# Removal keys' norms over 72 columns, and small matmuls tied behind the main passes in a two-layer RWKV-7 decoder kernel

## Chip, cores and metric

The kernel runs on one core of a Trainium2 chip. The metric is the device time of one execution in microseconds. TensorE (PE) does the matmuls and loads their weights (PEld), VectorE (DVE), ScalarE (ACT) and GpSimd (POOL) the elementwise work, and SyncE (SP) issues most transfers.

## The reference

Two layers are applied to 288 tokens: a prompt of 256 and eight samples of 4. Each layer is a half-step SwiGLU feed-forward block, a mixer, and another feed-forward block, each behind an RMS norm with shift, scale and gate from a conditioning vector. The mixer adds a causal pooling branch and an RWKV-7 branch. What matters here is how RWKV-7 normalises its removal keys, one vector of 64 for each token and each of eight heads, and then runs its recurrence:

```python
kk = hs((k * k_k).astype(f32))
kk = kk / jnp.maximum(jnp.sqrt(jnp.sum(kk * kk, axis=-1, keepdims=True)), 1e-12)
...
S = S * w_t[:, :, None, :] + sa[..., None] * b_t[:, :, None, :] + v_t[..., None] * k_t[:, :, None, :]
y = jnp.einsum('bhvk,bhk->bhv', S, r_t)
```

Here `a_t` is minus the normalised key and `b_t` the normalised key times `a`.

## The kernel before

**Layout.** Features lie on the 128 partitions and the 288 tokens along the free axis. A width of 512 is four tiles, so one tile holds two heads, and `HP` is 4. The prompt is worked on in four chunks of 64 tokens.

**Main passes.** Every large product is made of weight tiles of 128x128 from one list (`weight_order`). `split_strip` takes four tiles at a time and splits each weight into a high part `wh` (ACT, L225) and a low part `wl` (DVE, L226). `mm3` (L251) then runs three matmuls a tile: `wh` by the high and by the low part of the data, and `wl` by the high part. They are called main passes below. Each is tied behind the one before by `tc.issue_after(self.last.ins)`, so among themselves they run in the order of the list. Results land in PSUM tiles `psmm` (three) and `pswk` (four). One list step of the mixer (`step`) is two weight tiles, that is six main passes.

**The planner.** The program is written as one sequence, and a planner then lays it out on the engines by its own durations: on each engine the earliest written instruction that it takes to be ready goes next. `tc.high_priority(offset=75)` moves the splits, and the evictions of the mixer's main passes, 75 instructions ahead in that ranking. An engine runs its list strictly in the planned order; where a true duration is longer than the planned one, it waits.

**The mixer.** It weaves two sequences. The main sequence (`main_ops`) holds the projections left after the first five tiles, the gates and the branch products. The other holds small products: low-rank weights (L814), squared norms of the removal keys (L835), their spread over the partitions of a head (`head_spread`, L819), scores (L906), transposes (L918), a triangular inverse (DVE, L937 to L949, then L1196 and L1208), the chunk recurrence (L1268 to L1286), outputs (L1244, L1248) and their group norm, and the final transposes (L1255). Small products go to `pswk` tiles, and nothing ties them to main passes: the planner may place them ahead of main passes written earlier, or behind ones written later.

`fill()` takes its next count from `PLAN` and runs that many items: first from a queue, then, where that is empty, main steps. `add` puts a small product into the queue with three main steps behind it. The counts are used up in this order: one at L829, four in the loop of the key norms (L836), one each at L846, L894, L1183, L1192, L1204 and L1211, then two in each of four chunks (L1270, L1282; entries 11 to 18), then entry 19 at L1304, behind `outputs(1)` of the last half of the prompt, and four at L1312. At the end of chunk 1, nine entries are added to an empty queue (L1297 to L1300). What follows the chunks is

```python
outputs(1)
fill()
while queue:
    fill(1)
need(10)
...
transposed(1)
```

where `fill(1)` takes one item and no entry of `PLAN`.

**The key norms.** For each `j` of four tiles ACT squares the keys, and a matmul with `hs` (128x32; column `e` sums the 64 rows of head `e`) writes 32 rows of one PSUM tile, of which two are used, by 288 tokens. ACT takes the root of the whole tile into `rn` (L838), DVE the maximum with 1e-12 (L839) and the reciprocal (L843), each on 128 partitions by 288 columns. Then `head_spread(rn, j)` multiplies by `hb` (32x128) and gives each head's value to its 64 partitions, from which DVE forms the scaled keys `AR` and `BK` (L878 to L891). `head_spread` serves the bonus sums `bsum` as well. The scores (L906) read `AR` and `BK`, and DVE masks them into `MM` (L910). Evictions of main passes by DVE (L668) and the splits of `wl` (L226) are queued between all of these.

Of the kernel before, what the change touches and what calls it, by code (L numbers as in the profile page):

```python
# [20 lines left out]
AF = mybir.ActivationFunctionType  # L21
# [4 lines left out]
P = 128  # L26
# [6 lines left out]
NT = TP + NS  # L33
DEPTH = 2
H = 8
HP = 4
# [32 lines left out]
WEAVE = 3  # L69
PLAN = (1, 0, 0, 11, 1, 15, 14, 18, 5, 6, 2, 0, 12, 13, 4, 4, 3, 9, 13, 1, 2, 8, 4, 2, 3, 0, 5, 1, 1, 7)  # L70
FIRST = 3
# [65 lines left out]
for _n, _w in PARAMS:  # L137
# [3 lines left out]

CONSTS = [("ones", 1), ("eps", 1), ("ident", 128), ("mhalf", 1), ("hs", 32), ("hb", 128),
          ("maskp", 128), ("masks", 64), ("bmask", 8), ("id32", 32), ("id16", 16), ("halves", 2), ("scan", 288),
# [8 lines left out]
def make_consts():  # L152
# [6 lines left out]
    p = np.arange(P)  # L159
    put("ident", np.eye(P, dtype=np.float32))  # L160
    put("mhalf", np.full((P, 1), -0.5, np.float32))
    put("ones", np.ones((P, 1), np.float32))
    hs = np.zeros((P, 32), np.float32)
    hb = np.zeros((P, P), np.float32)
    for e in range(2):
        hs[64 * e:64 * e + 64, e] = 1.0
        hb[e::32, 64 * e:64 * e + 64] = 1.0
    put("hs", hs)
    put("hb", hb)
    s, t = p % 64, np.arange(64)  # L170
    put("maskp", np.stack([s[:, None] < t, s[:, None] <= t], 1).astype(np.float32))
    s, t = p % 32, np.arange(32)
# [14 lines left out]


class Kernel:
    def __init__(self, ctx, tc, io):  # L190
        self.ctx, self.tc, self.nc, self.io = ctx, tc, tc.nc, io
        self.order = weight_order()
        self.wpos = 0
        self.nstrips = len(self.order) // STRIP
        self.raw, self.hl = {}, {}
        self.next_slot, self.next_split = 0, 0
        self.psn = 0
        self.last = None

    def pool(self, name, bufs=1, **kw):  # L200
# [54 lines left out]

    def ps_wk(self):
        return self.p_wk.tile([P, 512], F32, tag="wk", name="pswk")

# [364 lines left out]
    def mixer(self, l):  # L623
        nc = self.nc
        tc = self.tc
        V, S, G, T = nc.vector, nc.scalar, nc.gpsimd, nc.tensor
        self.mod_close()
# [9 lines left out]
        def tj(name):  # L637
            return tl([P, NT], "tj", name, bufs=3)
# [18 lines left out]
        rks = tl([P, HP, 32], "rks")  # L657
        G.tensor_tensor(out=rks, in0=self.cst("hs").unsqueeze(1).to_broadcast([P, HP, 32]),
                        in1=self.par(l, "r_k").unsqueeze(2).to_broadcast([P, HP, 32]), op=ALU.mult)
        V.tensor_scalar(ka1, self.par(l, "k_a"), -1.0, 1.0, op0=ALU.mult, op1=ALU.add)  # L660
        ident, hs, hb = self.cst("ident"), self.cst("hs"), self.cst("hb")

# [154 lines left out]
        def head_spread(rows, j):  # L817
            ps = self.ps_wk()
            T.matmul(ps[:, :NT], hb[32 * j:32 * j + 32, :], rows[32 * j:32 * j + 32, :], start=True, stop=True)  # L819
            return ps[:, :NT]  # L820

        halves = [slice(0, 64), slice(64, 128)]
        quarter = [slice(32 * g, 32 * g + 32) for g in range(4)]
# [6 lines left out]
        kps = self.ps_wk()  # L830
        for j in range(HP):
            lora_mm(j)
            t = tl([P, NT], "tj", "kk2", bufs=3)
            S.activation(out=t, in_=xk[:, j, :], func=AF.Square, scale=self.par(l, "k_k", j))
            T.matmul(kps[32 * j:32 * j + 32, :NT], hs, t, start=True, stop=True)  # L835
            fill()  # L836
        rn = tj("rn")
        S.activation(out=rn, in_=kps[:, :NT], func=AF.Sqrt)  # L838
        V.tensor_scalar(rn, rn, 1e-12, None, op0=ALU.max)  # L839
# [36 lines left out]
        for j in range(HP):  # L876
            ps = head_spread(rn, j)
# [5 lines left out]
        for j in range(HP):  # L883
            t = tj("ka")
# [55 lines left out]
        for s in range(30, 0, -1):  # L940
            t0 = (s + 1) // 2
            n = 16 - t0
# [44 lines left out]
        out = []  # L987
# [205 lines left out]
        ps = self.ps_wk()  # L1193
        for u in range(16):
            for q in range(2):
                T.matmul(ps[hi[q], 32 * u:32 * u + 32], MU[lo[q], u, q, 0, 32:64], Tc[lo[q], u, :],  # L1196
                         start=True, stop=True)
# [7 lines left out]
        ps = self.ps_wk()  # L1205
# [8 lines left out]
        for q in range(2):  # L1214
            ps = self.ps_wk()
# [7 lines left out]
            n = 1 + q  # L1223
# [285 lines left out]
```

## Time and profile before

| | us |
|---|---|
| median of 3 runs | 1427.91 |
| the three runs | 1427.98, 1427.91, 1426.09 |
| profiled execution | 1426.15 |
| its span, first to last instruction | 1424.4 |
| PE busy in it | 1379.7 |
| DVE busy | 958.6 |
| ACT busy | 724.4 |

The profile comes from one execution. Its span leaves out 1.75 us around the first and last instruction. An engine's idle time is listed just before the instruction that ended it, with the instruction elsewhere that released it. The end of a matmul is modelled, so lines of PE overlap. A matmul of plain f32 data appears as two records; a main pass is one. PEclk is the granted clock of PE as a share of 2.4 GHz.

### The profile page before, as it was taken

The numbers are of one execution on the slowest core, as the hardware profiler recorded it, in microseconds if no ns is written. First come the engines' busy times: TensorE is split into PE (matmuls) and PEld (weight loads), VectorE is DVE, ScalarE is ACT, GpSimd is POOL, SyncE is SP. The second block draws the span as 40 slices with busy tenths as digits, with TensorE's granted clock in tenths as the row PEclk, the third lists the DMA queues.
The fourth block names the chain that finished last, engine by engine and source line by source line (L and its number), as shares of the span: only waits on it lengthen the run. The fifth ranks groups of instructions, "written<-read, shape, count | busy, mean of one in ns | idle before, by whom it ended". The sixth has DMA issues, their size and how long they took to land.

```text
span 1424.4 us, 28726 instructions
## 1 busy us (share of the span) xinstructions
PE 1379.7 (97%) x11280; PEld 1286.5 (90%) x11280; DVE 958.6 (67%) x2071; ACT 724.4 (51%) x1466; POOL 106.8 (7%) x151
## 2 busy tenths in 40 slices
PE   6999999999999999999999999999999999999997
PEld 5989999988888999899999899997897889999997
DVE  4644556899867885455677555669996678755554
ACT  4444444686534664444455445457654356555532
POOL 0000002000112010000211000110001210100012
PEclk9999999999999999999999999999998999999999
DMA  8878865543323776887667644554341247445552
GB/s 363 312 267 308 296 237 179 183 148 113 100 92 135 253 255 221 303 302 264 244 212 273 238 148 163 165 187 143 114 145 63 90 153 276 154 163 163 165 172 97
DMA packets 70264, 279.74 MB, mean 196 GB/s; under 512 B 9328, under 2 KB 11504, under 8 KB 60784
## 3 DMA queue, kind: packets, MB, share of 16 engines
q1 hardware_dynamic: 66384, 274.33, 54.7%
q10 hardware_dynamic: 3744, 3.57, 0.9%
q8 instruction: 88, 1.44, 0.4%
q14 instruction: 48, 0.39, 0.1%
HBM read 273.64 MB, written 4.23 MB: 195 GB/s over the span
## 4 chain that ended last, share of the span: by engine, by line
PE 86%; DVE 9%; issue 2%; DMA 1%; ACT 1%; POOL 1%; POOLq 0%; DVEq 0%; ACTq 0%; SPq 0%
PE psmm L251 44%; PE pswk L251 30%; PE psmd L315 4%; DVE wl L226 2%; PE pswk L918 1%; DVE xn L495 1%; DMA raw<-in_wflat 1%; DVE ul L498 0%; DVE pw L688 0%; POOL gn L1128 0%; DMA shs<-in_shift 0%; PE pswk L1273 0%; PE pswk L814 0%; DVE MM L910 0%; DMA cc<-in_c 0%
## 5 line engine op out<-in xcount | busy, mean ns | idle before, releaser
L226 DVE TENSOR_TENSOR wl<-raw,wh 128x512 fp32r<-128x512 f32 x732 | 512.4, 702 | 331.5 <-ACT wh L225 323.9
L225 ACT CAST wh<-raw 128x512 fp32r<-128x512 f32 x732 | 452.8, 620 | 543.1 <-PE psmm L251 284.6
L251 PE MATMUL psmm<-uh,wh 128*128 128x288 f32 x1072 | 324.2, 302 | 1.2 <-ACT uh L506 1.2
L251 PE MATMUL psmm<-ul,wh 128*128 128x288 f32 x1072 | 320.0, 298 | 0.4 <-DVE ul L507 0.3
L251 PE MATMUL psmm<-uh,wl 128*128 128x288 f32 x1072 | 319.4, 298 | 1.0 <-DVE wl L226 1.0
L251 PEld LDWEIGHTS psmm<-uh,wh 128*128 128x128 f32 x1072 | 203.6, 190 | 13.0 <-issue 8.2
L251 PEld LDWEIGHTS psmm<-uh,wl 128*128 128x128 f32 x1072 | 204.0, 190 | 4.7 <-issue 2.6
L251 PEld LDWEIGHTS psmm<-ul,wh 128*128 128x128 f32 x1072 | 203.9, 190 | 3.9 <-issue 2.3
L251 PE MATMUL pswk<-ul,wh 128*128 128x288 f32 x608 | 179.7, 296 | 0.0
L251 PE MATMUL pswk<-uh,wh 128*128 128x288 f32 x608 | 179.7, 296 | 0.0
L251 PE MATMUL pswk<-uh,wl 128*128 128x288 f32 x608 | 179.6, 295 | 0.0
L251 PEld LDWEIGHTS pswk<-uh,wh 128*128 128x128 f32 x608 | 114.7, 189 | 5.4 <-issue 4.2
L251 PEld LDWEIGHTS pswk<-ul,wh 128*128 128x128 f32 x608 | 114.7, 189 | 0.0
L251 PEld LDWEIGHTS pswk<-uh,wl 128*128 128x128 f32 x608 | 114.6, 189 | 0.0
L251 PE MATMUL pswk<-hl,wh 128*128 128x288 f32 x352 | 103.8, 295 | 0.0
L251 PE MATMUL psmm<-hl,wh 128*128 128x288 f32 x352 | 103.8, 295 | 0.0
L251 PE MATMUL psmm<-hh,wl 128*128 128x288 f32 x352 | 103.8, 295 | 0.0
L251 PE MATMUL pswk<-hh,wl 128*128 128x288 f32 x352 | 103.7, 295 | 0.0
L251 PE MATMUL psmm<-hh,wh 128*128 128x288 f32 x352 | 103.7, 295 | 0.0
L251 PE MATMUL pswk<-hh,wh 128*128 128x288 f32 x352 | 103.2, 293 | 0.0
L315 PE MATMUL psmd<-modw,csilu 128*32 128x512 f32 (+2 forms) x832 | 70.6, 481 | 9.1 <-DMA modw<-in_wmod 9.1
L378 POOL TENSOR_TENSOR sq<-x 128x288 f32<-128x288 f32 x28 | 19.8, 708 | 770.1 <-DVE x L533 770.1
(321 smaller groups left out, 2379.3 us busy)
## 6 DMA issues: line engine op xcount, KB each, us to landing
raw<-in_wflat SPq DMA_DIRECT2D x366, 512.0 KB, 3.4
modw<-in_wmod SPq DMA_DIRECT2D x72, 1024.0 KB, 7.3
s<-in_wkv SPq DMA_DIRECT2D x4, 512.0 KB, 6.7
o_wkvs<-s SPq DMA_DIRECT2D x4, 512.0 KB, 2.7
x<-in_x SPq DMA_DIRECT2D x1, 1152.0 KB, 5.4
o_y<-yo SPq DMA_DIRECT2D x2, 288.0 KB, 2.5
o_y<-yo ACTq DMA_DIRECT2D x2, 288.0 KB, 2.6
o_pool<-po SPq DMA_DIRECT2D x8, 67.5 KB, 2.7
```

The lines of the kernel that those rows point to most:

```text
L225: self.nc.scalar.copy(wh, src)
L226: self.nc.vector.tensor_tensor(out=wl, in0=src, in1=wh.bitcast(F32), op=ALU.subtract)
L251: self.last = self.nc.tensor.matmul(ps, w, x, start=start and n == 0, stop=stop and n == 2)
L315: mm = nc.tensor.matmul(self.mod_ps[32 * q:32 * q + 32, :size], self.csilu[:, k, :], w[:, kk, q, :], start=(k == 0), stop=(k == KD - 1))
L378: nc.gpsimd.tensor_tensor(out=t, in0=x, in1=x, op=ALU.mult)
L495: nc.vector.scalar_tensor_tensor(out=t, in0=self.x[:, k, :TP], scalar=g1, in1=r[:, :TP], op0=ALU.mult, op1=ALU.mult)
L918: T.transpose(ps[:n, 128 * hp:128 * hp + 128], src(hp), ident)
```

## The change

The squared norms are gathered in quarters. The 288 tokens are cut into four runs of 72, and run `t` of tile `j` goes to rows `2t` and `2t + 1` of the 32 rows of `j`, so that eight rows by 72 columns hold what two rows by 288 held. Four matmuls with four forms of `hs` add up in the same PSUM columns. Root, maximum and reciprocal then work on 72 columns. `head_spread` picks the rows of each run with four forms of `hb`; for `bsum`, which is 288 wide, it makes one matmul as before. The constants grow by 96 and 384 columns.

In the mixer, `T` becomes an `Ordered` object: the first matmul or transpose after each new `pswk` tile is tied behind the last main pass written so far. Entry 19 of `PLAN` goes from 1 to 6.

```diff
@@ -67,7 +67,7 @@
 SLOT = 8
 PRIO = 75
 WEAVE = 3
-PLAN = (1, 0, 0, 11, 1, 15, 14, 18, 5, 6, 2, 0, 12, 13, 4, 4, 3, 9, 13, 1, 2, 8, 4, 2, 3, 0, 5, 1, 1, 7)
+PLAN = (1, 0, 0, 11, 1, 15, 14, 18, 5, 6, 2, 0, 12, 13, 4, 4, 3, 9, 13, 6, 2, 8, 4, 2, 3, 0, 5, 1, 1, 7)
 FIRST = 3
 RMS = {0: 0.25, 1: 0.15, 2: 0.25}
 SPREAD = {0: 0.45, 1: 0.4, 2: 0.45}
@@ -139,7 +139,7 @@
     _o += _w
 NPAR = _o
 
-CONSTS = [("ones", 1), ("eps", 1), ("ident", 128), ("mhalf", 1), ("hs", 32), ("hb", 128),
+CONSTS = [("ones", 1), ("eps", 1), ("ident", 128), ("mhalf", 1), ("hs", 128), ("hb", 512),
           ("maskp", 128), ("masks", 64), ("bmask", 8), ("id32", 32), ("id16", 16), ("halves", 2), ("scan", 288),
           ("rc", 64)]
 COFF, _o = {}, 0
@@ -160,11 +160,12 @@
     put("ident", np.eye(P, dtype=np.float32))
     put("mhalf", np.full((P, 1), -0.5, np.float32))
     put("ones", np.ones((P, 1), np.float32))
-    hs = np.zeros((P, 32), np.float32)
-    hb = np.zeros((P, P), np.float32)
-    for e in range(2):
-        hs[64 * e:64 * e + 64, e] = 1.0
-        hb[e::32, 64 * e:64 * e + 64] = 1.0
+    hs = np.zeros((P, 4, 32), np.float32)
+    hb = np.zeros((P, 4, P), np.float32)
+    for t in range(4):
+        for e in range(2):
+            hs[64 * e:64 * e + 64, t, 2 * t + e] = 1.0
+            hb[2 * t + e::32, t, 64 * e:64 * e + 64] = 1.0
     put("hs", hs)
     put("hb", hb)
     s, t = p % 64, np.arange(64)
@@ -186,6 +187,27 @@
     return c
 
 
+class Ordered:
+
+
+    def __init__(self, kernel):
+        self.k = kernel
+
+    def _issue(self, f, *args, **kw):
+        k = self.k
+        if not k.fresh or k.last is None:
+            return f(*args, **kw)
+        k.fresh = False
+        with k.tc.issue_after(k.last.ins):
+            return f(*args, **kw)
+
+    def matmul(self, *args, **kw):
+        return self._issue(self.k.nc.tensor.matmul, *args, **kw)
+
+    def transpose(self, *args, **kw):
+        return self._issue(self.k.nc.tensor.transpose, *args, **kw)
+
+
 class Kernel:
     def __init__(self, ctx, tc, io):
         self.ctx, self.tc, self.nc, self.io = ctx, tc, tc.nc, io
@@ -196,6 +218,7 @@
         self.next_slot, self.next_split = 0, 0
         self.psn = 0
         self.last = None
+        self.fresh = False
 
     def pool(self, name, bufs=1, **kw):
         return self.ctx.enter_context(self.tc.tile_pool(name=name, bufs=bufs, **kw))
@@ -254,6 +277,7 @@
         return self.p_mm.tile([P, 512], F32, tag="mm", name="psmm")
 
     def ps_wk(self):
+        self.fresh = True
         return self.p_wk.tile([P, 512], F32, tag="wk", name="pswk")
 
     def ps_any(self):
@@ -623,7 +647,7 @@
     def mixer(self, l):
         nc = self.nc
         tc = self.tc
-        V, S, G, T = nc.vector, nc.scalar, nc.gpsimd, nc.tensor
+        V, S, G, T = nc.vector, nc.scalar, nc.gpsimd, Ordered(self)
         self.mod_close()
         es = ExitStack()
         pl = es.enter_context(tc.tile_pool(name=f"mx{l}", bufs=1, reuse_waits="tile"))
@@ -655,10 +679,11 @@
         V.tensor_tensor(out=shs, in0=shs, in1=self.par(l, "mu").unsqueeze(2).to_broadcast([P, NPA, NB]), op=ALU.mult)
         V.tensor_scalar(mu1, self.par(l, "mu"), -1.0, 1.0, op0=ALU.mult, op1=ALU.add)
         rks = tl([P, HP, 32], "rks")
-        G.tensor_tensor(out=rks, in0=self.cst("hs").unsqueeze(1).to_broadcast([P, HP, 32]),
+        G.tensor_tensor(out=rks, in0=self.cst("hs")[:, 0:32].unsqueeze(1).to_broadcast([P, HP, 32]),
                         in1=self.par(l, "r_k").unsqueeze(2).to_broadcast([P, HP, 32]), op=ALU.mult)
         V.tensor_scalar(ka1, self.par(l, "k_a"), -1.0, 1.0, op0=ALU.mult, op1=ALU.add)
-        ident, hs, hb = self.cst("ident"), self.cst("hs"), self.cst("hb")
+        ident = self.cst("ident")
+        hs, hb = [self.cst(n).rearrange("p (t m) -> p t m", t=4) for n in ("hs", "hb")]
 
         def shifted(i, ps, dst):
 
@@ -816,7 +841,10 @@
 
         def head_spread(rows, j):
             ps = self.ps_wk()
-            T.matmul(ps[:, :NT], hb[32 * j:32 * j + 32, :], rows[32 * j:32 * j + 32, :], start=True, stop=True)
+            r = quarter[j]
+            n = rows.shape[1]
+            for t in range(NT // n):
+                T.matmul(ps[:, n * t:n * t + n], hb[r, t, :], rows[r, :], start=True, stop=True)
             return ps[:, :NT]
 
         halves = [slice(0, 64), slice(64, 128)]
@@ -832,10 +860,13 @@
             lora_mm(j)
             t = tl([P, NT], "tj", "kk2", bufs=3)
             S.activation(out=t, in_=xk[:, j, :], func=AF.Square, scale=self.par(l, "k_k", j))
-            T.matmul(kps[32 * j:32 * j + 32, :NT], hs, t, start=True, stop=True)
+            for i in range(4):
+                T.matmul(kps[32 * j:32 * j + 32, :NT // 4], hs[:, i, :], t[:, NT // 4 * i:NT // 4 * (i + 1)],
+                         start=i == 0, stop=i == 3)
             fill()
-        rn = tj("rn")
-        S.activation(out=rn, in_=kps[:, :NT], func=AF.Sqrt)
+
+        rn = tj("rn")[:, :NT // 4]
+        S.activation(out=rn, in_=kps[:, :NT // 4], func=AF.Sqrt)
         V.tensor_scalar(rn, rn, 1e-12, None, op0=ALU.max)
         for j in range(HP):
             V.tensor_tensor_scan(out=cs[:, j, :], data0=self.cst("scan"), data1=sig[:, j, :], initial=0.0,
```

## Rows read from the trace of the kernel before

**Rows 1.** The page: busy time by engine; the chain that ended last

```profile
PE 1379.7 (97%) x11280; PEld 1286.5 (90%) x11280; DVE 958.6 (67%) x2071; ACT 724.4 (51%) x1466; POOL 106.8 (7%) x151
PE 86%; DVE 9%; issue 2%; DMA 1%; ACT 1%; POOL 1%; POOLq 0%; DVEq 0%; ACTq 0%; SPq 0%
```

**Rows 2.** Windows, layer 0: us; PE, PEld, DVE, ACT, POOL busy; clock; DMA

```profile
283.00:334.00 51.00, 47.50 (x354) 40.23 (x353) 49.85 (x124) 37.08 (x80) 1.04 (x2) 1.00 0.41 131
```

**Rows 3.** Lines, DVE: operation, shapes, count | busy us, mean ns

```profile
L413 DVE RECIPROCAL rb<-rb 128x144 f32<-128x144 f32 x10 | 9.8, 1020 | 0.6 <-ACT rb L409 0.6
L843 DVE RECIPROCAL rn<-rn 128x288 f32<-128x288 f32 x2 | 3.9, 1946 | 0.0
L839 DVE TENSOR_SCALAR rn<-rn 128x288 f32<-128x288 f32 x2 | 0.6, 304 | 0.0
```

**Rows 4.** Timeline, PE, scores of layer 0: start, us, instruction [idle before <-releaser]

```profile
320.50 0.29 PE L251 MATMUL psmm<-ul,wh 128*128 128x288 f32 x1
322.41 1.16 PE L906 MATMUL pswk<-AR,BK 64*128 64x128 f32 x16 [1.62 <-DVE AR L888]
324.08 0.40 PE L251 MATMUL psmm<-uh,wl 128*128 128x288 f32 x1 [0.51 <-DVE wl L226]
...
325.38 0.29 PE L251 MATMUL psmm<-uh,wl 128*128 128x288 f32 x1
325.60 2.06 PE L906 MATMUL pswk<-AR,BK 64*128 64x128 f32 x32
...
329.50 0.40 PE L251 MATMUL psmm<-uh,wh 128*128 128x288 f32 x1
...
330.68 0.65 PE L981 MATMUL pswk<-rkk,rks 128*32 128x288 f32 x2 [0.64 <-DVE rkk L975]
```

**Rows 5.** Timeline of DVE at layer 0's scores

```profile
321.05 1.22 DVE L888 TENSOR_TENSOR AR<-xr,ep 128x1024 f32<-128x1024 f32 x1
...
322.92 0.51 DVE L668 SCALAR_TENSOR_TENSOR sgl<-psmm,par,sgl 128x287 f32<-128x287 f32 x1
323.35 0.68 DVE L226 TENSOR_TENSOR wl<-raw,wh 128x512 fp32r<-128x512 f32 x1
```

**Rows 6.** Timeline of PE, layer 0: small products of f32

```profile
285.84 0.67 PE L835 MATMUL pswk<-kk,consts 128*32 128x288 f32 x2
...
310.04 0.77 PE L819 MATMUL pswk<-rn,consts 32*128 32x288 f32 x8
...
424.79 1.04 PE L1248 MATMUL pswk<-S,AR 128*64 128x128 f32 x8
...
436.25 1.10 PE L1244 MATMUL pswk<-UV,MM 128*64 128x64 f32 x32
```

**Rows 7.** Windows around falls of the clock, columns as in rows 2

```profile
373.30:376.60 3.30, 3.30 (x101) 2.96 (x101) 2.66 (x9) 3.20 (x6) 0.99 (x2) 1.00 0.12 19
...
1018.40:1021.70 3.30, 3.30 (x18) 3.02 (x20) 3.01 (x6) 1.06 (x2) 0.00 (x0) 0.53 0.18 29
...
1066.20:1069.50 3.30, 3.30 (x72) 3.12 (x72) 3.21 (x8) 1.52 (x3) 0.53 (x1) 0.53 0.04 11
1069.60:1079.70 10.10, 10.10 (x161) 8.85 (x162) 3.23 (x9) 4.22 (x8) 0.99 (x2) 0.50 0.17 54
```

**Rows 8.** Timeline of PE, both layers: stalls and what follows

```profile
370.62 1.20 PE L1196 MATMUL pswk<-Tc,MM 32*32 32x32 f32 x64 [1.78 <-DVE Tc L1189]
...
447.68 0.63 PE L1255 MATMUL pswk<-consts,yn 128*128 128x128 f32 x4 [2.79 <-DVE yn L1129]
...
1016.65 1.16 PE L906 MATMUL pswk<-AR,BK 64*128 64x128 f32 x16 [1.62 <-DVE AR L888]
...
1024.99 0.40 PE L251 MATMUL psmm<-uh,wh 128*128 128x288 f32 x1
...
1066.12 1.77 PE L1196 MATMUL pswk<-Tc,MM 32*32 32x32 f32 x64 [1.81 <-DVE Tc L1189]
...
1148.19 1.02 PE L1255 MATMUL pswk<-consts,yn 128*128 128x128 f32 x4 [2.78 <-DVE yn L1129]
```

## The prediction

> **What bounds the kernel now.** I read the page first: TensorE (PE) is busy for 1379.7 of 1424.4 us and makes 86% of the chain that ended last [rows 1]. So a change pays in three ways only: PE work removed, PE idle time filled, or PE time spent at the lower clock avoided. Work taken from VectorE (DVE) or ScalarE (ACT) counts where PE waits for it. The busy times by stretch come second. From 283 to 334 us, where layer 0's mixer builds its keys and scores, DVE is busy 49.85 of 51.0 us while PE has holes [rows 2]: here DVE decides. Third, the timeline around the changed lines. In layer 0 PE ends its main pass at 320.50 + 0.29 = 320.79, idles 1.62 us until DVE has written `AR` (L888), runs one score product (L906, sixteen matmuls), idles 0.51 us for a split weight `wl` (L226), runs ten main passes and then the second product [rows 4]. DVE takes its work in the order L888, L668, L226; that split ends at 323.35 + 0.68 = 324.03, just ahead of the pass that waited for it [rows 5]. Both idle times stand in layer 1 as well (the first shown in [rows 8]).
>
> Last, the clock. In layer 1 the granted clock is 0.53 from 1018.40, after that stall, and 0.53 and 0.50 from 1066.20 to 1079.70, after a stall of 1.81 us ahead of L1196; these are the lower level, 1.2 GHz [rows 7, 8]. The same stalls in layer 0, of 1.62 and 1.78 us, are followed by 1.00 [rows 2, 4, 7, 8]. A stall of this length may cost a fall or not; where it lies seems to matter, and so a shift of some us can trade one fall for another.
>
> **The norms over 72 columns.** The change puts the squared norms of 288 tokens into 72 columns, so three operations shrink. The reciprocal (L843) takes 1946 ns on 288 columns, and 1020 ns on 144 columns at L413 [rows 3]: 6.4 ns a column, so 72 columns give an estimate of 1020 - 72 x 6.4 = 557 ns, and 1.39 us are saved. The maximum (L839) takes 304 ns on 288; I take off 0.1 us. The root on ACT lies ahead of a queue that isn't full; I take 0. DVE does 1.5 us less in each layer, in the stretch where it is the bound.
>
> PE pays for it. Each of four key squares makes one product of two matmuls (L835), 0.67 us, and all four spreads of the result (L819) take 0.77 us [rows 6]; both become four pieces of 72 columns. That is 32 and 32 matmuls in place of 8 and 8. No row shows 72 columns, so bounds: below, nothing, because the columns add up to the same and 64-column matmuls come at 1.10 / 32 = 34 ns each; above, 128-column matmuls come at 1.04 / 8 = 130 ns each [rows 6], and 64 x 0.13 = 8.3 us stand against 4 x 0.67 + 0.77 = 3.45, so +4.9 us a layer. 72 is nearest to 64 columns, so I take +0.5 us. Where it falls matters more: both groups come before PE's wait at 320.79, which DVE ends, so up to 1.8 us of it (the wait worked out below) is hidden by that wait. I take 0 on the end; without that cover it is +0.5 a layer, at most +4.9.
>
> A rule speaks against this step. The Trainium skill, page "TensorE: Matmul & The Clock Gate", section "Back-to-back issue gap", says that the spacing of matmuls in a stream is set by the weight load as well, and gives 81 ns for 128 columns. Taken as a floor, 64 matmuls would cost 5.2 us against 3.45, an estimate of +1.7 us a layer. The 34 ns of the 64-column rows disagrees with it as a floor; those use different halves of the array side by side, which the new pieces don't. By the rule and without cover, the forecast below would be 3.5 us higher, 1428.0, which belongs to the first rival.
>
> The constants grow by 480 columns, 240 KB more in one load that is issued behind the first gates of the first layer, most of a feed-forward layer ahead of its first use. Transfers of all kinds are 1% of the chain [rows 1], and what hides this one is that layer. I take 0; without that cover it delays the weight loads behind it by a fraction of that 1%.
>
> **The tie of small products.** The first matmul after each new small PSUM tile must now follow the last main pass written before it. Counting passes in code and trace, only the first score product stands ahead of its written place, by the ten passes of [rows 4]; every other small product of both mixers already has as many passes ahead of it as the code writes, or more. So the tie acts there alone. It doesn't simply fill the hole: the ten passes want `wl`, and DVE splits it behind L888 and L668. PE will wait at 320.79 for `wl`. With DVE 1.5 us ahead, `wl` comes at 322.53 and the first pass at 322.58, an idle time of 1.79 instead of 1.62 + 0.51. From first pass to score product it is 325.60 - 324.08 = 1.52 us, and a product takes 2.06 / 2 = 1.03, so the second product starts at 322.58 + 1.52 + 1.03 = 325.13 instead of 325.60: 0.47 us gained a layer. What DVE waits for later, the first masking (L910), comes after 324.10 + 1.16 instead of 322.41 + 1.16; queued behind it are the other maskings and the bonus products, but further `wl` splits can go in that time, which now stand between the maskings. If that lets DVE run ahead, the 0.64 us that PE waits for `rkk` [rows 4] shrinks; bounds 0 and 0.64, I take 0.3.
>
> The stall is then one piece of 1.8 us, and in layer 1 begins some 0.5 us earlier for what layer 0 gained. I take it that the fall at 1018.40 goes. It costs (1024.99 - 1016.65) - (329.50 - 322.41) = 1.25 us [rows 4, 8].
>
> **More steps behind the outputs.** `PLAN[19]` goes from 1 to 6 at the `fill()` behind `outputs(1)`. The queue holds items there: nine entries with three steps each make 36, the four fills since took 4, 3, 9 and 13, so 7 are left. `fill` takes from the queue first, and the loop right behind empties it. One and then six, or six and then one, give the same sequence: this edit does nothing. The waits of 2.79 and 2.78 us for `yn` ahead of `transposed(1)` [rows 8] stay.
>
> **The sum.** -2 x (0.47 + 0.3) - 1.25 = -2.8 us. The profiled run took 1426.15 (span 1424.4 and 1.75 around it), so 1423.35. It is the second lowest of the four times known; the three runs shown average 1427.3, 1.2 above it, and the median is 1427.91. I forecast 1424.5, likely between 1422.5 and 1426.5. About 0.2%, 2.9 us, is what a measurement can tell from no change, so this lies just on the faster side.
>
> **Rivals.**
> *No net gain:* DVE's order leaves `wl` at about 323.0, and then the tie gives nothing, or the pieces are not covered and take back what it gives (2 x 0.5 up to 2 x 4.9). For it: DVE evicts main passes (L668) between the key steps, and those come at PE's pace, not earlier. Against: DVE has hardly any idle time to lose. About 1427.3. Chance 0.17.
>
> *The longer wait, slower:* the tie takes from PE the only work it had. If DVE's saving doesn't reach the split, `wl` stays at 324.03, the second product starts at 324.08 + 1.52 + 1.03 = 326.63, 1.03 late, the maskings and all behind them up to as much again, and a hole of 3.3 us brings the lower clock in layer 0 too, 1.25. From 1426.15: +2 x 2.06 + 1.25 = +5.4, with the 1.2 above 1432.7. It decides from `wl` at 325.60 - 1.52 - 1.03 - 0.05 = 323.0 on, that is if less than 1.0 of the 1.5 us arrives. Chance 0.15.
>
> *The long fall goes too:* the stall ahead of L1196 in layer 1 (1.81 us) shifts as in layer 0 and brings no fall. From L1196 to L1255 layer 0 takes 447.68 - 370.62 = 77.06 us and layer 1 1148.19 - 1066.12 = 82.07 [rows 8]: 5.0 us, so 1419.5. For it: the same stall without a fall stands in layer 0. Against: the shift must be of the right size, and layer 0 must not catch one. Chance 0.18.
>
> *The long fall comes to layer 0 as well:* the same mechanism the other way, +5.0, 1429.5. Chance 0.10. The skill's page above, section "Part 1: The HAM clock gate", says that the gate runs free of the kernel's start, by which neither trade could be told beforehand; the four times within 1.9 us rather speak for falls that come back at the same places.
>
> *The edit of the plan works:* were the queue shorter than I count, the tail waits would go, 2 x 2.79, giving 1418.9. Chance 0.04.
>
> **Chances.** The forecast has 0.36, about 0.22 of it under the bound for faster. Faster: 0.22 + 0.18 + 0.04 = 0.44. Same: 0.14 + 0.17 + 0.05 of the new fall = 0.36. Slower: 0.15 + 0.05 = 0.20. A range of 1418.5 to 1431.5 holds all but the longer wait beyond it and a spot at the low end.
>
> **What would show it.** L843 near 0.56 us and 72 columns in L838 and L839. In each layer no main pass between the first two score products, one wait of about 1.8 us for `wl` instead of two waits, and the second product about 0.5 us earlier. L835 and L819 four times as many, without PE waiting longer. The waits of 2.8 us ahead of the second L1255 unchanged in both layers. A clock of 1.00 after layer 1's scores. The forecast is wrong if `wl` comes after 323.0, if the planner, with other durations, moves main passes elsewhere, or if the long fall goes or doubles.

## The result, and the profile after

The changed kernel takes 1435.96 us (median of 7 runs, 1431.97 to 1436.59) against 1426.09 us beside it (7 runs, 1419.26 to 1427.98): ratio 1.0080, 95% interval 1.0057 to 1.0102. It is slower, by 9.9 us by the medians and 11.4 by the ratio; 1424.5 was forecast, and the time lies above the range. The profiled execution took 1436.44 us. First its page (busy time by engine) and the cores' view (span, mean granted clock):

```profile
PE 1389.1 (97%) x11376; PEld 1299.7 (91%) x11376; DVE 955.3 (67%) x2071; ACT 725.7 (51%) x1466; POOL 105.6 (7%) x151
```

```profile
core 0: 1434.7 us, clock 0.984
```

PE is busy 9.4 us longer than in [rows 1], so the loss isn't idle time alone: there is more work on PE, or it runs slower, and both will show. The timeline of PE at layer 0's spread (start, us, instruction), between two main passes:

```profile
312.52 0.29 PE L274 MATMUL psmm<-uh,wl 128*128 128x288 f32 x1
312.74 0.44 PE L202 MATMUL pswk<-rn,consts 32*128 32x72 f32 x2
313.02 0.49 PE L199 MATMUL pswk<-rn,consts 32*128 32x72 f32 x3
...
314.48 0.89 PE L199 MATMUL pswk<-rn,consts 32*128 32x72 f32 x8
315.30 0.40 PE L274 MATMUL psmm<-uh,wh 128*128 128x288 f32 x1
```

All small products of the mixer now carry the lines of the tie's helper (L202 with a tie, L199 without), so they are told by their tiles. The 32 matmuls of the spread take PE from 312.74 to 315.30, 2.56 us or 80 ns each, against 0.77 us for eight before [rows 6]. The key squares, cut into quarters just the same, took 0.67 us a product [rows 6] and now read

```profile
288.26 0.69 PE L199 MATMUL pswk<-kk,consts 128*32 128x72 f32 x8
```

So cutting by itself costs little. What DVE does behind it (line L249 is the split of `wl`, L693 the eviction of main passes, L919 the product `AR`):

```profile
318.68 0.69 DVE L249 TENSOR_TENSOR wl<-raw,wh 128x512 fp32r<-128x512 f32 x1 [0.98 <-ACT wh L248]
...
321.30 0.52 DVE L693 SCALAR_TENSOR_TENSOR xv<-psmm,par,xv 128x287 f32<-128x287 f32 x1 [1.83 <-ACT sho L692]
...
326.82 1.22 DVE L919 TENSOR_TENSOR AR<-xr,ep 128x1024 f32<-128x1024 f32 x1
...
328.36 0.68 DVE L249 TENSOR_TENSOR wl<-raw,wh 128x512 fp32r<-128x512 f32 x1
```

DVE, full in [rows 2], now idles 2.8 us, because it waits, by way of ACT, for main passes that PE delivers later: behind the pieces, and then at the lower clock (the window from 315.50 below). In the trace of pieces_only (the pieces alone, see below), where the clock doesn't fall there, DVE idles 1.35 and 0.57 us ahead of two evictions in this stretch. And PE at the scores and further on, with the waits that the tie and the outputs have (views of the timeline, by window; the rows from 1029.61 on are layer 1's scores):

```profile
329.10 0.40 PE L274 MATMUL psmm<-uh,wl 128*128 128x288 f32 x1 [2.21 <-DVE wl L249]
331.59 0.58 PE L202 MATMUL pswk<-AR,BK 64*128 64x128 f32 x1
...
375.82 0.21 PE L202 MATMUL pswk<-Tc,MM 32*32 32x32 f32 x1 [2.56 <-DVE Tc L1220]
...
458.96 0.35 PE L202 MATMUL pswk<-consts,yn 128*128 128x128 f32 x1 [2.79 <-DVE yn L1160]
...
1029.61 0.40 PE L274 MATMUL psmm<-uh,wl 128*128 128x288 f32 x1 [2.21 <-DVE wl L249]
...
1031.13 0.37 PE L202 MATMUL pswk<-AR,BK 64*128 64x128 f32 x1
...
1032.12 0.27 PE L202 MATMUL pswk<-AR,BK 64*128 64x128 f32 x1
```

In place of 1.62 and 0.51 us [rows 4] there is one wait of 2.21 us; the wait ahead of the products out of `Tc`, 1.78 and 1.81 us [rows 8], has grown to 2.56; that ahead of the last transposes is what it was. The windows view (us, busy time of PE, PEld, DVE, ACT, POOL, granted clock, DMA) shows what follows:

```profile
315.50:318.80 3.30, 3.30 (x16) 3.30 (x16) 2.32 (x9) 1.17 (x2) 0.00 (x0) 0.53 0.48 140
329.20:332.50 3.30, 3.30 (x18) 3.02 (x20) 2.60 (x6) 1.06 (x2) 0.00 (x0) 0.53 0.39 104
377.00:390.50 13.50, 13.50 (x200) 11.56 (x202) 6.02 (x14) 7.32 (x13) 1.74 (x3) 0.51 0.24 80
...
1029.20:1032.50 3.30, 2.89 (x34) 2.73 (x36) 3.30 (x8) 0.96 (x2) 0.00 (x0) 1.00 0.25 49
1076.70:1090.20 13.50, 13.50 (x210) 11.56 (x210) 5.80 (x14) 7.20 (x14) 1.60 (x3) 0.51 0.27 80
```

Two falls to the lower level in layer 0 that [rows 2] did not have, and the long fall behind the products out of `Tc` in both layers, where before only layer 1 had it [rows 7]. The first of the two falls, at 315.50, follows the pieces of the spread: PE had not waited before it. The fall behind layer 1's scores, at 1018.40 before, is gone, as forecast: PE's wait there now begins at 1027.40, and the clock behind it is 1.00. Before the mixer there is one more loss: the vector that mixes in the shifted inputs waits for its load (view of the tile `shs`: idle time of its engine until the transfer, and the time from issue to landing):

```profile
  DMA shs<-in_shift: 4.1, 1
...
DMA to landing us min/median/max: 6.7/6.7/6.7
```

The same view of the kernel before reads 1.7 and 4.4 us; layer 0's first products come 2.1 us later by it.

### The profile page after: what moved, and what is told of

Read it like the earlier page. It is cut to its first block, busy times and chain, and to the rows that moved or that the text cites. A ratio compares the mean times of both kernels' runs of the same rounds, so it can differ in the third digit from the quotient of the medians.

```text
span 1434.7 us, 28916 instructions
## 1 busy us (share of the span) xinstructions
PE 1389.1 (97%) x11376; PEld 1299.7 (91%) x11376; DVE 955.3 (67%) x2071; ACT 725.7 (51%) x1466; POOL 105.6 (7%) x151
## 3 DMA queue, kind: packets, MB, share of 16 engines
q8 instruction: 89, 1.46, 0.4%
## 4 chain that ended last, share of the span: by engine, by line
PE 87%; DVE 6%; DMA 2%; issue 2%; ACT 1%; POOL 1%; POOLq 0%; ACTq 0%; DVEq 0%; SPq 0%
PE psmm L274 45%; PE pswk L274 31%; PE pswk L199 5%; PE psmd L339 4%; PE pswk L202 2%; DVE wl L249 1%; DMA shs<-in_shift 1%; POOL gn L1159 0%; DVE xn L519 0%; DVE pw L713 0%; DVE ul L522 0%; DMA cc<-in_c 0%; DMA raw<-in_wflat 0%; DVE MM L941 0%; DVE prod L976 0%
## 5 line engine op out<-in xcount | busy, mean ns | idle before, releaser
L249 DVE TENSOR_TENSOR wl<-raw,wh 128x512 fp32r<-128x512 f32 x732 | 511.8, 701 | 332.7 <-ACT wh L248 325.0
```

Source lines behind the costliest of these rows:

```text
L249: self.nc.vector.tensor_tensor(out=wl, in0=src, in1=wh.bitcast(F32), op=ALU.subtract)
```

## Two measures for the experiments

The kernel before, run beside the experiments, took 1416.5 to 1435.0 us in 149 runs, and each run lists its mean granted clock, 0.982 to 0.997. The times lie on a line: 1424.1 us at 0.990, and 1.03 us more for each 0.001 less, with a scatter of 1.1 us. So each kernel gets two numbers: the mean clock of its runs, and how far they stand from that line, "at equal clock" (standard error 0.3 to 0.5 us; that of a mean clock is 0.0002 to 0.0013). The expectations were written while the line rested on fewer runs.

| kernel | median us (before beside it) | ratio, 95% | mean clock | at equal clock |
|---|---|---|---|---|
| before, 149 runs | 1423.6 | | 0.9906 | 0 |
| changed | 1436.0 (1426.1) | 1.0080, 1.0057 to 1.0102 | 0.9837 | +4.5 |
| pieces_only | 1426.6 (1422.1) | 1.0027, 1.0009 to 1.0045 | 0.9929 | +5.4 |
| norms_only | 1428.6 (1422.1) | 1.0042, 1.0018 to 1.0067 | 0.9877 | +2.2 |
| tie_only | 1428.4 (1422.1) | 1.0032, 1.0007 to 1.0057 | 0.9855 | -1.7 |
| one_spread | 1430.6 (1422.1) | 1.0045, 1.0024 to 1.0065 | 0.9843 | -0.1 |
| consts_only | 1426.6 (1422.3) | 1.0020, 0.9999 to 1.0042 | 0.9898 | +2.4 |
| after_p8 | 1432.2 (1422.3) | 1.0055, 1.0033 to 1.0076 | 0.9855 | +2.9 |
| tail_steps | 1414.8 (1422.3) | 0.9955, 0.9934 to 0.9977 | 0.9941 | -3.5 |
| tie_covered | 1418.3 (1422.3) | 0.9959, 0.9936 to 0.9983 | 0.9891 | -7.1 |
| early6 | 1425.0 (1424.1) | 1.0024, 1.0002 to 1.0046 | 0.9886 | +0.9 |
| narrow | 1422.3 (1424.1) | 0.9984, 0.9962 to 1.0006 | 0.9907 | -1.4 |
| consts512 | 1426.9 (1424.1) | 1.0017, 0.9994 to 1.0040 | 0.9902 | +1.4 |
| tail4 | 1413.9 (1424.1) | 0.9938, 0.9913 to 0.9962 | 0.9927 | -6.0 |
| after_again | 1428.8 (1423.3) | 1.0048, 1.0027 to 1.0069 | 0.9880 | +3.7 |
| tie_again | 1425.4 (1423.3) | 1.0021, 1.0001 to 1.0041 | 0.9870 | -1.1 |
| narrow_tail | 1416.9 (1423.3) | 0.9952, 0.9931 to 0.9973 | 0.9907 | -7.1 |
| robin | 1419.6 (1425.0) | 0.9969, 0.9952 to 0.9987 | 0.9932 | -0.7 |
| after_robin | 1426.3 (1425.0) | 1.0019, 1.0005 to 1.0033 | 0.9880 | +0.1 |
| after_mended | 1419.4 (1425.0) | 0.9962, 0.9946 to 0.9977 | 0.9884 | -6.6 |

The changed kernel's 4.5 us at equal clock and its lower clock, 0.0069 x 1.03 / 0.001 = 7.1 us, make 11.6; its ratio of 1.0080 is 11.4 us.

## The experiments

### The parts alone: pieces, norms, tie

The first theories: A, the small pieces of the spread are the loss, for nothing covers them; B, the tie is.

```diff
# pieces_only: the kernel before, its spread of rn in four pieces
-            T.matmul(ps[:, :NT], hb[32 * j:32 * j + 32, :], rows[32 * j:32 * j + 32, :], start=True, stop=True)
+            n = NT if rows is bsum else NT // 4
...
+            for t in range(NT // n):
+                T.matmul(ps[:, n * t:n * t + n], hb[r, :], rows[r, n * t:n * t + n], start=True, stop=True)
# norms_only: the changed kernel without the tie
-        V, S, G, T = nc.vector, nc.scalar, nc.gpsimd, Ordered(self)
+        V, S, G, T = nc.vector, nc.scalar, nc.gpsimd, nc.tensor
# tie_only: the kernel before with class Ordered, and T = Ordered(self)
# one_spread: the changed kernel, DVE widens rn to 288 columns first
+        V.tensor_tensor(out=wide.rearrange("p (t c) -> p t c", t=4), in0=rn.unsqueeze(1).to_broadcast([P, 4, NT // 4]),
+                        in1=self.cst("hq").unsqueeze(2).to_broadcast([P, 4, NT // 4]), op=ALU.mult)
...
+            T.matmul(ps[:, :NT], (ha if rows is wide else hb[:, 0, :])[r, :], rows[r, :], start=True, stop=True)
```

> The kernel before, with the spread of rn cut into four matmuls of 72 columns each, and nothing else. Theory A (the pieces are the loss: PE pays for them, nothing covers it, because DVE's chain waits for PE's main passes in turn): the spread takes about 2.6 us of PE in place of 0.8, the main pass behind it starts 1.9 us later in each layer, and the time rises by 3 to 4 us, more where the stretch is followed by the lower clock. Theory B (the tie is the loss, the pieces are covered by PE's later wait): the time stays within 1 us and the wait ahead of the first score product shrinks.

> The changed kernel without the tie of small products. Theory A: +1 to +4 us against before, and up to 5 more with a further fall of the clock, since 1.9 us a layer are paid for the spread and the shorter reciprocal gives back at most 1.5. Theory B: no slower than before, 0 to -3 us, since the longer reciprocal is gone and the two waits at the scores shrink.

> The kernel before with the tie of small products alone. Theory A: the two waits at the scores (1.62 and 0.51 us) become one wait of 2 to 3.5 us for wl; the main passes behind come between 1 us earlier and 1 us later in each layer, so -2 to +3 us with the clock's share. Theory B: +6 to +10 us, as in the changed kernel.

> The changed kernel, except that DVE widens the 72 columns to 288 once (a multiplication by a mask of run against row) and the spread of rn is one matmul of 288 columns a tile again, as before the change. Theory A: the 1.9 us a layer at the spread go, so 4 us and a fall of the clock less than the changed kernel: -4 to +2 us against before. Theory B: as the changed kernel, +6 to +10 us.

Neither theory is enough: by the ratios the pieces alone cost 3.8 us, the norms with their pieces 6.0 and the tie alone 4.6, so none makes the whole, and tie_only lies between what A and B expected. By the two measures they part: the pieces cost work (+5.4, at an undisturbed clock), the tie gains work (-1.7) and lowers the clock (0.9855). The +5.4 are more than the 3.7 us that the spread of both layers takes; pieces_only's profile has two more waits, of 0.93 and 0.70 us, at the norm behind layer 1's mixer, and whether its other runs have them isn't known. The one row of the pieces in the timeline of pieces_only, and the one wait in tie_only's:

```profile
310.23 2.63 PE L822 MATMUL pswk<-rn,consts 32*128 32x72 f32 x32
```

```profile
322.05 0.40 PE L273 MATMUL psmm<-uh,wl 128*128 128x288 f32 x1 [3.29 <-DVE wl L248]
```

The wait of 3.29 us is the "hole of 3.3 us" of the rival with the longer wait. With the tie the products out of `Tc` also stand elsewhere: the instruction lists have them behind main pass 2178 of the span, where the kernel before has 2188. The ten passes that the tie sets ahead of the scores are taken from in front of these products, and in tie_only and one_spread they wait 2.56 us too.

### Constants

```diff
-CONSTS = [..., ("hs", 32), ("hb", 128),
+CONSTS = [..., ("hs", 32), ("hb", 128), ("more", 480),      # consts512: 512
```

> The kernel before with 480 more columns in its late load of constants, which nothing reads. Theory C (the longer constants delay the row of shifted inputs, which three of the kernels that carry them show some 2 us late at the first products of layer 0, once per execution): 1.5 to 2.5 us slower than before beside it, and the gap at the first products stays at 1.15 us but stands later. Rival (the start of the span wanders by as much between executions of any kernel): no difference, within 1 us.

> The kernel before with 512 unused columns of constants in place of 480: the tiles behind them keep their old place within 2048 bytes. Theory E (it is the place of the following tiles, or of their parts, that makes the 60 KB of shifted inputs land after 6.7 us instead of 4.4): the transfer lands after 4.4 us again, and the time at equal clock is that of the kernel before. Rival (it is the amount): 6.5 to 7 us and 2 us over, as with 480.

consts_only stands 2.4 us from the line, and its view of the tile `shs` reads as that of the changed kernel:

```profile
DMA to landing us min/median/max: 6.7/6.7/6.7
```

In consts512 it is 7.8 us, so theory E falls. In all profiles 60 KB of shifted inputs land after 4.3 to 4.8 us with constants as before and after 5.8 us or more with longer ones. Their load is issued some 210 us ahead of this transfer; how it delays it stays open.

### Covering the stalls

```diff
# after_p8: the changed kernel, four more queue items ahead of the products out of Tc (entry 19 is 1 again)
-PLAN = (1, 0, 0, 11, 1, 15, 14, 18, 5, ...
+PLAN = (1, 0, 0, 11, 1, 15, 14, 18, 9, ...
# tail_steps: the kernel before, two main steps ahead of the last transposes (tail4: four)
         while queue:
             fill(1)
+        fill(2)
         need(10)
# tie_covered: tie_only with both edits
```

> The changed kernel with four more queue items written ahead of the products out of Tc (PLAN's ninth entry 5 becomes 9). Theory D (the tie makes these products wait 2.56 us instead of 1.8 with nothing written behind, and the long fall of the clock follows that stall in both layers, 13.65 us at half rate, worth some 5 to 6 us each where before only one layer had it): the stall falls under 1 us, both long falls go, the mean clock rises from 0.984 to about 0.992 and the time falls by 7 to 11 us to 1425 to 1429. Theory A (the time is lost to the small pieces' own issue and to DVE behind them): the stall goes but the time falls by its own 2 x 2 us at most, to 1432 or more.

> The kernel before with two main steps (12 passes, 1.6 us) put between the drained queue and the last four transposes of the outputs, whose wait is 2.79 us in each layer and is followed by 3.41 us at half clock. Theory D (a fall follows a stall of that length): the wait falls to 1.2 us, both falls go, and the time falls by 2.5 to 4 us. Rival (the steps are only moved from behind the transposes, where they cover the split of the gated values): the same wait appears at the first main pass that reads the split, and the time stays within 1 us.

> The kernel before with four main steps (24 passes, 3.2 us) ahead of the last transposes, where two left a wait of 1.20 us. If the wait is all that the place costs: no wait there, 1 to 2 us under the version with two. If the cover of the split behind it runs out (one step is left): a wait at the first main pass that reads the split, and no gain or a loss against the version with two.

> The kernel before with the tie alone, and with both covers: four more queue items ahead of the products out of Tc and two main steps ahead of the last transposes. Theory D: the tie's own gain (one wait at the scores in place of two, 1.6 us per layer before the clock) shows once the falls at these stalls are gone: 1414 to 1419, 3 to 8 us under before beside it, mean clock 0.993 or more. Theory A's reading of the tie (it is a loss by itself, as tie_only was 6 us over before): no faster than before, 1420 or more.

after_p8 missed: its stall is still there (first row below, timeline of PE). By its trace the products stand behind main pass 2175, so the edit brought no more passes in front of them; why the planner left them there isn't settled. tie_covered has the same edit, the same wait of 2.65 us and a clock of 0.9891 where 0.993 was expected. Its 1418.3 us lie in the range that theory D gave, but by the tail's cover alone. So no run here shortens the stall ahead of the products out of `Tc` under the tie. The tail did what theory D said, and more. The timeline of tail4 has no wait at L1255 (second fence), and the clock behind it is 1.00 in both layers (third, windows):

```profile
375.88 0.21 PE L202 MATMUL pswk<-Tc,MM 32*32 32x32 f32 x1 [2.65 <-DVE Tc L1220]
```

```profile
447.45 0.60 PE L1255 MATMUL pswk<-consts,yn 128*128 128x128 f32 x4
```

```profile
448.00:451.00 3.00, 3.00 (x25) 3.00 (x24) 2.97 (x8) 1.35 (x4) 0.00 (x0) 1.00 0.72 254
...
1137.00:1140.00 3.00, 3.00 (x25) 3.00 (x24) 2.96 (x7) 1.36 (x4) 0.00 (x0) 1.00 0.77 276
```

The edit of `PLAN[19]` makes no such steps: the changed kernel's wait there is 2.79 us as before. By its ratio tail4 is the fastest version here, 0.9938 of the kernel before.

### Which stall lowers the clock with the tie

```diff
# early6: the kernel before, products out of Tc seven passes earlier (self.passes counts the main passes)
+            after = self.early.ins if self.passes in (2182, 6574) else self.last.ins    # early: last product out of Tc
-            with self.tc.issue_after(self.last.ins):
+            with self.tc.issue_after(after):
# after_again: the changed kernel (tie_again: tie_only, 20 times), ahead of the scores' wait
+            for _ in range(14 if self.passes in (1945, 6337) else 0):
+                with self.tc.issue_after(self.last.ins):
+                    self.last = self.nc.tensor.matmul(ps, w, x, start=True, stop=True)
```

> The kernel before with one thing moved: its products out of Tc stand seven main passes earlier in TensorE's order (behind pass 2181 instead of 2188, and the same in layer 1), nothing is tied and no work is added. Theory D (the tie's loss is this place: it puts these products behind pass 2178, the stall there becomes 2.56 us, and a long fall of the clock follows): the stall grows from 1.78 to some 2.7 us, 13.65 us at half clock follow in both layers, the mean clock of the runs falls from 0.992 to about 0.986 and the median rises by 5 to 9 us. Rival (the stall costs its own length only, and the low clock of the kernels with the tie comes from the scores): plus 0 to 2 us, clock unchanged.

> The changed kernel with the first pass of one group repeated 14 times (1.84 us, each repetition starts the group anew, so the sums are the same) in front of the wait for wl at the scores, in both layers. Theory F (the one long wait at the scores, 2.21 us, is what lowers the clock in the kernels with the tie, by itself and by what follows it): the wait falls to 0.4 us, no fall follows it, the mean clock rises from 0.984 to 0.987 or more and the time falls by 3 us or more against 1435, to 1432 or less. Rival D2 (the falls belong to the products out of Tc and what runs thin behind them): the wait is filled but the clock stays at 0.983 to 0.985 and the time at 1434 to 1437.

> The kernel before with the tie alone, and 20 repeated passes (2.6 us) in front of its wait of 3.29 us at the scores, in both layers. Theory F: mean clock from 0.9855 to 0.989 or more, time from 1427 to 1423 or less. Rival D2: clock and time as in tie_only.

early6 has the stall and in its profile the long falls, too (timeline of PE, then windows):

```profile
373.97 0.75 PE L1199 MATMUL pswk<-Tc,MM 32*32 32x32 f32 x28 [2.69 <-DVE Tc L1192]
```

```profile
374.10:387.60 13.50, 13.50 (x228) 11.97 (x227) 5.92 (x15) 6.23 (x11) 1.51 (x3) 0.51 0.12 41
1073.90:1084.00 10.10, 9.67 (x168) 8.60 (x170) 5.37 (x14) 5.07 (x9) 1.51 (x3) 0.51 0.09 24
```

But its runs have 0.9886 on the mean, a drop of 0.002, about twice its standard error, where 0.007 is to be explained, and the time rises by 3.4 us by the ratio, not 5 to 9. Theory D may be right in kind, but it is too large. after_again fills the other wait, and its timeline shows the repeated pass and what is left:

```profile
323.71 2.01 PE L277 MATMUL psmm<-uh,wh 128*128 128x288 f32 x14
...
326.35 0.40 PE L279 MATMUL psmm<-uh,wl 128*128 128x288 f32 x1 [0.37 <-DVE wl L250]
```

Though PE does 28 passes more, the clock rises to 0.9880 and the ratio falls from 1.0080 to 1.0048. So the scores' wait matters as theory F says. In tie_again the clock rose from 0.9855 to 0.9870 only, below what F asked and within the noise (standard errors 0.0011 and 0.0008). How the lost clock divides between the stalls isn't settled, and the stalls are not all of it: the next section's after_robin keeps both waits at 2.21 and 2.56 us and has 0.9880. What the 20 profiles show of PE's waits between 285 and 1400 us: of 56 of 2.5 us and more, 52 were followed by a fall within 2.2 us of their end; of 8 of 2.2 us, 3; of 58 of 1.4 to 1.9 us, 17; of 9 of 1.1 to 1.3 us, none.

### Does the narrower norm pay, and why pieces cost what they do

```diff
# narrow: norms_only with one_spread's widening (narrow_tail: hb as before, and fill(4) at the tail)
# robin: norms_only; after_robin: the changed kernel; the same pieces in another order
-        for j in range(HP):
-            ps = head_spread(rn, j)
+        pss = [self.ps_wk()[:, :NT] for _ in range(HP)]
+        n = NT // 4
+        for t in range(4):
+            for j in range(HP):
+                r = quarter[j]
+                T.matmul(pss[j][:, n * t:n * t + n], hb[r, t, :], rn[r, :], start=True, stop=True)
+        for j, ps in enumerate(pss):
# after_mended: after_robin with fill(4) at the tail
```

> The norms over 72 columns without the tie and without the small pieces of the spread: VectorE widens the 72 columns to 288 with a mask and each tile is spread by one product of 288 columns. Compared at equal clock (the runs of the kernel before lie on 1424.2 us at 0.990, minus 1.08 us per 0.001). The prediction's term (1.5 us of VectorE per layer reach the end, 3.0 in all) with the constants' 2.2 us: 0 to 1 us under the kernel before. Theory A2 (the gain is real, but the four pieces per tile eat it): under norms_only, which is 2.0 us over, by about 3.7 us, that is 1 to 2 us under the kernel before. Rival (VectorE's saving does not reach the end): 2 us over.

> The norms over 72 columns with one product of 288 columns per spread tile, constants longer by 228 columns instead of 612, no tie, and four main steps ahead of the last transposes. If the parts add up (narrow minus 1.5 at equal clock, of which its constants are plus 2.3 and a third of them remain; the four steps minus 6.0): 7.5 to 9 us under the kernel before at equal clock and 9 to 13 us under its median, 1409 to 1414. If the gain of the norms is gone once the tail is covered: as tail4, 1413 to 1416.

> The norms over 72 columns without the tie, as norms_only, with the sixteen pieces of the spread in another order: the first piece of all four tiles, then the second of all four, so that neighbours read different quarters of the 32 x 4 rows. Theory G (the price of 80 ns a piece is that of neighbours in the same quarter): the 32 matmuls take 1.2 us or less instead of 2.6, the main passes behind them come 1.4 us or more earlier in each layer, and at equal clock the kernel stands 2 to 3.5 us under norms_only, near narrow (minus 1.5). Rival (80 ns is the pace of any such stream of load and matmul): 2.5 us for the 32 and no difference from norms_only (plus 2.0).

> The changed kernel with the same order of the pieces as robin. Theory G: at equal clock plus 4.3 falls to about 0, near one_spread (minus 0.3), and the median from 1435 to 1429 to 1432, the clock staying near 0.984. Rival: 1433 to 1437 as before the edit.

> The changed kernel with the pieces in that order and four main steps ahead of the last transposes. Theory G with the tail's own gain (minus 6.1 at equal clock, and some 0.002 to 0.004 of clock): 6 us under the kernel before at equal clock, median 1418 to 1424. Rival (the pieces keep their price): 1424 to 1428.

narrow is 3.6 us better than norms_only at equal clock: without the pieces the gain is there. robin keeps all the pieces and lets neighbours read different quarters of the 32 x 4 rows. Its row in the timeline, to be held against 2.63 us above:

```profile
310.13 1.13 PE L912 MATMUL pswk<-rn,consts 32*128 32x72 f32 x32
```

35 ns a matmul. Nothing but the order differs (and that all four PSUM tiles are taken at once), and robin stands 2.9 us under norms_only, after_robin 4.4 us under the changed kernel, at equal clock. Theory G holds: the price of 80 ns was that of neighbours in the same quarter. The clock rises as well, which G had not expected: from 0.9877 to 0.9932 in robin and from 0.9837 to 0.9880 in after_robin. The windows view of after_robin has no fall behind the spread, to be held against 0.53 from 315.50 above:

```profile
313.60:317.00 3.40, 3.40 (x28) 3.40 (x27) 3.40 (x13) 1.52 (x3) 0.00 (x0) 1.00 0.70 250
```

The fall there stands in the three profiles that have the tie and the pieces in the old order (changed, after_p8, after_again) and in neither with the new order (after_robin, after_mended); norms_only and pieces_only, with the old order and no tie, don't have it either. So the order alone is worth 1.0080 - 1.0019 = 0.0061, some 8.7 of the changed kernel's 11.4 us (by the two intervals within some 3.7 us): about 4.4 of work and 4.4 of clock. after_mended brings the change with both mends (the order and the tail) to 0.9962, and narrow_tail to 0.9952, neither better than tail4 alone. narrow_tail misses its 1409 to 1414: at equal clock it is 1.1 us under tail4, within the error of both.

## Why the prediction was wrong, step by step

*The reciprocal and the maximum: right.* The lines view of DVE:

```profile
L874 DVE RECIPROCAL rn<-rn 128x72 f32<-128x72 f32 x2 | 1.2, 596 | 0.0
...
L870 DVE TENSOR_SCALAR rn<-rn 128x72 f32<-128x72 f32 x2 | 0.4, 192 | 0.0
```

596 ns for the estimated 557, and 1.46 us less per layer.

*The pieces: the step that failed.* "72 is nearest to 64 columns, so I take +0.5 us": the spread's 32 matmuls came at 80 ns, not 34, and the same main passes start 1.86 us later behind them, in both layers; the key squares add some 0.3 us from pass to pass, most of it waits. The prediction had itself named why the 64-column rows might not apply (they run side by side) and then applied them; robin shows 35 ns as soon as the pieces do run side by side. Nor are 80 ns the price of cutting. Two key-square matmuls of 288 columns took 0.67 us, and the eight pieces of 72 that replace them take 0.69. But the eight spread matmuls, with four times the columns of one key square, took only 0.77 us [rows 6]: the four tiles, each in its own quarter of the rows, ran side by side already. Setting the four pieces of one tile behind each other, that is eight matmuls in one quarter, gave this up. The Trainium skill, page "TensorE: Matmul & The Clock Gate", section "Back-to-back issue gap", gives about 81 ns for 128 columns in a stream of weight loads and matmuls; the 80 ns here lie at that figure, at 72 columns, and robin's 35 ns lie below it, with as many weight loads. The estimate of +1.7 us a layer that I worked out from it and set aside was near the measured 2.2, but the weight load isn't shown to be the reason: the order is.

*"I take 0 on the end", because PE's wait covers it: failed with it.* PE's lateness isn't taken up by the wait for DVE, since DVE in its turn waits for what PE delivers (the 0.98 and 1.83 us above). Of the 1.5 us that DVE saved, 0.3 arrived: it began `AR` 0.26 us after PE stopped [rows 4, 5], and 0.07 us before (326.82, with PE stopping at 329.10 - 2.21 = 326.89). norms_only, without the tie, gives the same: PE waits 1.30 us for `AR` in place of 1.62. And in pieces_only, which is only later by the pieces, that wait is 1.62 us as before: it covered nothing of them. The bound above, +4.9 us a layer uncovered, held; the range didn't use it.

*The constants: 0 taken, 2.4 us measured* (1.4 with 512 columns), by a way that no step considered.

*The tie: its kind right, two sizes off.* One wait in place of two, no main pass between the first two score products, and the wait for `rkk` gone, as said. The wait is 2.21 us, not 1.79, so of the 0.47 us at the second score product 0.1 came: in layer 1, at a clock of 1.00, it starts 4.72 us after PE stopped (1032.12 - 1027.40), and 4.81 before in layer 0 (325.60 - 320.79 [rows 4]). "So the tie acts there alone" is wrong: the products out of `Tc` moved ten passes forward and wait 0.75 us longer. tie_only's -1.7 us at equal clock are near the forecast's -2 x 0.77 by luck: there the first score product stands where the second stood before, 4.81 us after PE stopped (323.57 against 318.76), so nothing is gained at the scores and all of it behind them. And this gain and that of the norms are partly the same: either removes the wait for `wl` between the score products and most or all of that for `rkk` (0.17 us left in robin). With the constants' 2.4, narrower norms gain some 3.1 us without the tie (robin, -0.7) and some 0.6 with it, about the error of that difference (after_robin against tie_only: 0.1 + 1.7 - 2.4 = -0.6).

*The clock: the trade was mis-sized.* The fall at 1018.40 went, as forecast. That "the four times within 1.9 us rather speak for falls that come back at the same places" was wrong: 149 runs of one program spread over 18 us, with the clock. The Trainium skill's same page, section "Part 1: The HAM clock gate", calls the gate free of the kernel's start, and this fits it. What can be forecast is how readily a stall is followed by a fall, and the change lengthened two in each layer. Of the 7.1 us that the clock cost, after_robin gives back 4.4 by the order of the pieces alone, and after_again as much by filling the scores' wait; that is more than 7.1 together, so the two don't simply add, and how they divide is open. The prediction tied the clock to waits of PE only, and had no term for a fall behind the pieces.

*The edit of the plan: right.* With `PLAN[19]` = 6 alone the kernel before is the same list of instructions on every engine, and the waits of 2.79 us stayed.

*The rivals.* The longer wait was the nearest: it decides if less than 1.0 of the 1.5 us arrives, and 0.3 did; its 1432.7 lacks the pieces and the constants. The long fall in layer 0 came as well, which the prediction had named as a sign of being wrong.

## What to carry to other kernels

Before a matmul is cut into pieces, look at which rows of the array its neighbours use: the same 32 pieces took 2.63 us in one order and 1.13 in another. Compare versions at equal clock, and count their clock apart; a change that turns two short stalls into one long one can gain work and still lose time, as tie_only did (-1.7 us of work, ratio 1.0032). And where two engines feed each other in a loop, a wait of one for the other may cover no delay of its own: ask what the other is waiting for.

## What the hardware showed that I had not expected

- An unchanged program ran from 1416.5 to 1435.0 us, and 1.03 us per 0.001 of mean granted clock tells nearly all of it (scatter 1.1 us).
- Filling a stall with 28 passes of repeated work made the kernel faster, 1.0080 to 1.0048 of the kernel before, with the clock up from 0.9837 to 0.9880.
- Constants longer by 480 columns, loaded long before, made a 60 KB transfer land after 6.7 us instead of 4.4.
- The order of the same 32 matmuls, with neighbours in one quarter of the rows or in all four, was worth 8.7 us of a kernel of 1.4 ms, half of it by the clock.
